# A twenty-chunk ring for the channel mixers' activations in a hybrid GLA/FoX trunk on one Trainium2 core

## The chip, the cores and the metric

The kernel runs on one core of one Trainium2 chip, in one launch. Its time is in device microseconds (us); three runs gave 2291.82 us in the median (2291.04 to 2292.42). The core's engines are TensorE (PE; PEld is its weight load), VectorE (DVE), ScalarE (ACT), GpSimd (POOL) and SyncE (SP). Here SP issues the weight loads and POOL the transfers of the channel mixers' activations.

## The reference

A decoder trunk of two layers over 256 tokens with a width of 2048. Layer 0 mixes tokens with gated linear attention, layer 1 with forgetting attention; both also attend to 256 memory tokens. After either comes a channel mixer, which is what the change touches:

```python
def causal_dwconv(u, w, b):
    s_ = u.shape[1]
    up = jnp.pad(u, ((0, 0), (CONV_WIDTH - 1, 0), (0, 0)))
    return w[0] * up[:, 0:s_] + w[1] * up[:, 1:s_ + 1] + w[2] * up[:, 2:s_ + 2] + b

def conv_ffn(h, w_up, conv_w, conv_b, w_down):
    u = causal_dwconv(h @ w_up, conv_w, conv_b)
    a, val = split_cols(u, [FFN_HIDDEN, FFN_HIDDEN])
    return (jax.nn.silu(a) * val) @ w_down
...
        h = rmsnorm(x, norm_ffn[i])
        x = x + conv_ffn(h, ffn_w_up[i], ffn_conv_w[i], ffn_conv_b[i], ffn_w_down[i])
```

The hidden width is 5632, which is 44 chunks of 128 for the activated half `a` and 44 for `val`.

## The kernel before

**Precision.** Every float32 operand is split in two fp32r parts, a high one (a ScalarE cast) and a low one (a VectorE subtraction). A product is three matmuls: high by high, low by high, high by low. `split_unit` (line 214) does this to the weights: SP loads a unit of 128 x 1024 values (512 KB) into one of four `raw` buffers, ScalarE makes `whi` (line 230), VectorE makes `wlo` (line 231). The cast and the subtraction have their place in their engine's order well ahead of the matmuls (`high_priority(offset=AHEAD)`).

**Panels.** A panel is a block of columns of a weight matrix, consumed unit by unit. There are three ways to run one. `panel_tm` (line 313) is *narrow*: 512 columns, two 128-row chunks of the contraction to a unit, 12 matmuls of 128 x 512, two accumulators. `proj_tm` (line 276) does the same with other orders of the last units. `pair_tm` (line 353) is *wide*: 1024 columns, one contraction chunk to a unit, 12 matmuls, four accumulators (two halves of the tokens by two halves of the columns). In a wide panel a pair of contraction chunks can be done by the Strassen-Winograd scheme with seven products for eight: two units in 21 matmuls for 24, with extra casts (`split_more`, its cast in line 349), subtractions of weights (lines 399 to 402), a sum of the source made beforehand (`token_sums`, tiles `usum` and `dsum`), and an evacuation of four extra banks (`early`). A wide panel uses all eight PSUM banks if it has a Strassen pair; `flip` exchanges the four that its last units write (tiles `acc`) with the four others (`ps_o`, `ps_s`, `ps_t`), so that the following panel finds four free.

**The mixer** (`ffn`, line 1329). The 44 chunks come in three `PARTS`: 0 to 15, 16 to 31, 32 to 43. For each part the up panels run first, then the part's down panels, which add into the residual `x[0]` to `x[3]` (four column quarters of 512). An up pair (`up_pair`) is a wide panel that yields four chunks of both halves; its contraction has 16 chunks, its Strassen pair is the input chunks 4 and 5 (`SEVEN_UP`). Parts 0 and 1 are made of four up pairs each; part 2 of up pairs 32 and 36 and two narrow panels 40 and 42 (`up`), whose accumulators ScalarE evacuates at line 1440. The down panels of parts 0 and 1 are two wide ones with 16 units, Strassen pairs at the part's chunks 4 and 10 (`SEVEN_DOWN`); those of part 2 are one wide panel of 12 units without a Strassen pair for quarters 0 and 1, then a narrow one each for quarters 2 and 3 (`add_out`).

**A chunk's way from up to down** (`turn`). When an up panel ends, VectorE adds the last parts (line 1429) and transposes 32 x 32 blocks (line 1393). POOL writes the tile to DRAM (`far`, line 606) and reads it back in another order, four transfers per tile (line 611). Then six *steps* follow for every two chunks: four of three taps each (ScalarE, lines 1348 to 1350), one that adds them (VectorE, line 1357, and silu, line 1358), one that gates, splits into high and low part and, where needed, makes the sums for a Strassen pair (`gated`: VectorE line 1365, ScalarE line 487, VectorE line 488). The steps wait in a list, `waiting`. They are due eight ticks of a clock after the evacuation (seven in narrow panels), and `tick(most)` is called after every unit and issues at most `most` that are due: alternately one and two in up pairs, two in narrow and down panels. A down panel issues all that are left by its last units. Taps are placed behind the latest weight cast, gatings behind the latest low part (`issue_after`).

**Where the chunks lie.** In layer 0 the mixer's input is in `bufB` and its sixteen activation chunks in `bufA`; in layer 1 the other way round. A part's chunk j goes to buffer j - lo, so a part's activations overwrite those of the part before, and its up panels' steps come behind the earlier part's down panels.

**The order on the engines** is not only that of the code: the program is built with a planner that simulates times (`schedule_with_timeline_sim=True`) and orders each engine's instructions by simulated readiness and priority. On the chip each engine then runs its list in order.

**Around the mixers.** Layer 0's mixer is followed by `fox`: the finished quarters of `x` are transposed, written to DRAM by SP and read back (`land`), and split (`take`) as input of the next projections; in the mixer's last panel `land` and `take` come after its third, fourth, fifth and sixth unit. `mk[1]` and `mv[1]`, the memory keys and values of layer 1 (128 x 1024 float32 each), are made at the kernel's start and read in `fox` by `mem_parts(1, "B")`. In layer 1 the last mixer is followed by the final norm.

## Time and profile before

| | |
|---|---|
| median of three runs | 2291.82 us |
| the profiled execution | 2289.51 us |
| its span, first to last instruction | 2287.7 us |
| mean granted TensorE clock | 0.990 |
| busy: PE / DVE / ACT / POOL | 2230.5 / 1790.0 / 1416.9 / 124.3 us |
| matmuls | 10317 |
| DMA | 513.37 MB, 224 GB/s over the span |

The mixers take about 458 to 1190 us (layer 0) and 1525 to 2280 us (layer 1). In a row of windows the columns are: the window, its length, then for PE, PEld, DVE, ACT and POOL the busy time and (x) the number of instructions that lie in it, the granted TensorE clock, the busy share of the DMA engines, GB/s. In a row of the timeline: start, duration, engine, line, operation, out<-in, shapes, count, and in brackets the engine's idle time before it and what ended it. In a row of waits: who waited, for whom, us in total, how often, the longest. Names such as `A`, `B` and `mix` are the buffers of inputs and activations; `fvt`, `temp`, `yu`, `yzu` and `turn` are tiles on the chunks' way.

### The profile page before, as it was taken

The numbers are of one execution on the slowest core, as the hardware profiler recorded it, in microseconds if no ns is written. First come the engines' busy times: TensorE is split into PE (matmuls) and PEld (weight loads), VectorE is DVE, ScalarE is ACT, GpSimd is POOL, SyncE is SP. The second block draws the span as 40 slices with busy tenths as digits, with TensorE's granted clock in tenths as the row PEclk, the third lists the DMA queues.
The fourth block names the chain that finished last, engine by engine and source line by source line (L and its number), as shares of the span: only waits on it lengthen the run. The fifth ranks groups of instructions, "written<-read, shape, count | busy, mean of one in ns | idle before, by whom it ended". The sixth has DMA issues, their size and how long they took to land. (4 is left out here: it accounts for less than half of the span.)

```text
span 2287.7 us, 30031 instructions
## 1 busy us (share of the span) xinstructions
PE 2230.5 (97%) x10317; PEld 1861.7 (81%) x10317; DVE 1790.0 (78%) x2639; ACT 1416.9 (62%) x2258; POOL 124.3 (5%) x235
## 2 busy tenths in 40 slices
PE   9999999999999999999999999999999999999997
PEld 7888888878778887788778998887777888778885
DVE  7769986688898789878677569677888878987866
ACT  6655665557865676656665455455876567765674
POOL 0000000001000001000100000000000000100110
PEclk9999999999999999999999999999999999999998
DMA  9776658867675776656777767676776577756673
GB/s 350 224 224 212 207 178 257 248 224 229 229 241 175 231 253 229 189 202 222 227 240 247 215 203 246 206 245 214 234 240 217 183 230 247 239 193 220 223 257 129
DMA packets 166593, 513.37 MB, mean 224 GB/s; under 512 B 20636, under 2 KB 43816, under 8 KB 166440
## 3 DMA queue, kind: packets, MB, share of 16 engines
q1 hardware_dynamic: 151080, 464.51, 62.5%
q0 software_dynamic: 14784, 46.15, 6.4%
q8 instruction: 81, 1.33, 0.2%
q10 hardware_dynamic: 576, 0.79, 0.1%
q14 instruction: 72, 0.59, 0.1%
HBM read 468.63 MB, written 42.74 MB: 224 GB/s over the span
## 5 line engine op out<-in xcount | busy, mean ns | idle before, releaser
L231 DVE TENSOR_TENSOR wlo<-raw,whi 128x1024 fp32r<-128x1024 f32 (+4 forms) x734 | 866.9, 1196 | 321.8 <-ACT whi L230 300.4
L230 ACT ACTIVATE whi<-raw 128x1024 fp32r<-128x1024 f32 (+4 forms) x734 | 746.9, 1036 | 464.6 <-PE acc L334 183.9
L334 PE MATMUL acc<-whi,B 128*128 128x512 f32 (+3 forms) x1376 | 323.8, 372 | 0.0
L334 PEld LDWEIGHTS acc<-whi,B 128*128 128x128 f32 x1376 | 251.2, 188 | 32.9
L349 ACT ACTIVATE whi<-raw 128x1024 fp32r<-128x1024 f32 (+1 forms) x144 | 136.6, 952 | 208.3 <-PE acc L374 73.4
L374 PE MATMUL acc<-whi,mix 128*128 128x512 f32 x850 | 222.9, 396 | 9.4 <-ACT fvt L1440 3.9
L350 DVE TENSOR_TENSOR wlo<-raw,whi 128x1024 fp32r<-128x1024 f32 (+1 forms) x144 | 155.7, 1084 | 67.5 <-ACT whi L349 61.5
L374 PE MATMUL acc<-whi,B 128*128 128x512 f32 x730 | 191.9, 395 | 11.1 <-ACT B L487 9.3
L374 PEld LDWEIGHTS acc<-whi,mix 128*128 128x128 f32 x850 | 161.6, 191 | 45.2 <-ACT fvt L1440 4.3
L334 PE MATMUL acc<-wlo,B 128*128 128x512 f32 (+3 forms) x688 | 176.1, 371 | 0.0
L374 PEld LDWEIGHTS acc<-whi,B 128*128 128x128 f32 x730 | 138.6, 191 | 42.0 <-ACT B L487 10.1
L334 PEld LDWEIGHTS acc<-wlo,B 128*128 128x128 f32 x688 | 126.7, 188 | 16.9
L1357 DVE TENSOR_TENSOR tap<-tap,tap 128x1024 f32<-128x1024 f32 x88 | 107.5, 1221 | 28.6 <-ACT tap L1349 20.2
L374 PE MATMUL acc<-wlo,mix 128*128 128x512 f32 x425 | 123.2, 395 | 0.1
L374 PE MATMUL acc<-wlo,B 128*128 128x512 f32 x365 | 106.0, 393 | 0.1
L374 PEld LDWEIGHTS acc<-wlo,mix 128*128 128x128 f32 x425 | 81.0, 191 | 17.8 <-DVE wlo L350 0.7
L374 PE MATMUL ps_s<-whi,B 128*128 128x512 f32 x342 | 93.8, 390 | 0.0
L374 PE MATMUL ps_s<-whi,mix 128*128 128x512 f32 x334 | 93.1, 391 | 0.0
L334 PE MATMUL acc<-whi,mix 128*128 128x512 f32 x336 | 84.1, 390 | 0.0
L374 PEld LDWEIGHTS acc<-wlo,B 128*128 128x128 f32 x365 | 69.2, 190 | 15.0 <-DVE wlo L350 0.5
L374 PEld LDWEIGHTS ps_s<-whi,B 128*128 128x128 f32 x342 | 64.2, 188 | 13.5
L374 PEld LDWEIGHTS ps_s<-whi,mix 128*128 128x128 f32 x334 | 63.0, 189 | 13.4
(425 smaller groups left out, 3783.1 us busy)
## 6 DMA issues: line engine op xcount, KB each, us to landing
raw<-wp SPq DMA_DIRECT2D x743, 512.0 KB, 4.6
raw<-wp SPq DMA_DIRECT2D x32, 384.0 KB, 3.5
far<-yu POOLq DMA_DIRECT2D x22, 512.0 KB, 3.8
far<-yzu POOLq DMA_DIRECT2D x22, 512.0 KB, 3.8
fvt<-far POOLq DMA_DIRECT2D x80, 128.0 KB, 3.0
yzu<-far POOLq DMA_DIRECT2D x80, 128.0 KB, 3.5
raw<-wp SPq DMA_DIRECT2D x24, 388.0 KB, 3.9
far<-blk SPq DMA_DIRECT2D x12, 512.0 KB, 4.9
```

Source lines behind the costliest of these rows:

```text
L230: casts.append(S.activation(hi[:, s], raw[:, s], AF.Copy))
L231: lows.append(V.tensor_tensor(lo[:, s], raw[:, s], hi[:, s].bitcast(F32), ALU.subtract))
L334: mm = TE.matmul(acc[b][:, :n], src[kc - base][:, part, b * P : (b + 1) * P], ready[low][:, j * n : (j + 1) * n], start=i == low == part = ...
L349: casts.append(S.activation(hi[:, :n], src, AF.Copy))
L350: lows.append(V.tensor_tensor(lo[:, :n], src, hi[:, :n].bitcast(F32), ALU.subtract))
L374: r = TE.matmul(bank[name], x, w, start=name not in begun, stop=last)
L1357: V.tensor_tensor(t, t, taps[n][:, :, :, :T], ALU.add)
```

## The change

The activations get twenty buffers for sixteen: chunk j goes to buffer j modulo 20. In layer 1 the four added ones are new tiles. In layer 0 they are the tiles of `mk[1]` and `mv[1]`: POOL writes these to DRAM (`parked`) before the mixer, and at the start of `fox` reads them back into the same places.

The order of the panels changes. After part 0's last up pair the first up pair of part 1 runs, then the two down panels of part 0; after part 1's last pair the first of part 2, then part 1's down panels. Up pairs and down panels are generators now, driven one unit at a time; after every unit of either alternately one or two steps are issued, and the rule that issues all that are left is gone. In part 2 the narrow up panels 40 and 42 become a wide up pair 40. Its down panels are interleaved by hand: eight units of the wide one, four of the narrow one for quarter 2, the last four of the wide one, the last two of the narrow one; quarter 3 follows as before. The Strassen pair of up panels moves from input chunks 4, 5 to 6, 7.

```diff
-WIDE = ((0, 4, 8, 12), (16, 20, 24, 28), (32, 36))
-SEVEN_UP = (4,)
+RING = 20
+SEVEN_UP = (6,)
...
+            for t, tag, far in ((mk, "mk1", parked[0]), (mv, "mv1", parked[1])):
+                t[1] = const.tile(list(t[1].shape), F32, name=tag + "again", tag=tag)
+                nc.gpsimd.dma_start(t[1].rearrange("p a b -> p (a b)"), far)
...
-            def gated(i, seven):
+            def gated(j):
...
-                        split(m, i + s, r[:, s, :])
-                    if seven:
-                        sums[i] = held("dsum", i)
-                        token_sums(r, sums[i])
+                        split(m, (j + s) % RING, r[:, s, :])
+                    if j < PARTS[-1][0] and j % 16 in SEVEN_DOWN:
+                        sums[j] = held("dsum", j % 16)
+                        token_sums(r, sums[j])
...
-                for f in (0,) if end else (0, 2):
-                    count[2] += 1
-
-                    def hook(k):
-                        tick(2)
-                        if k in (hi - lo - 5, hi - lo - 3):
-                            left = 6 if k == hi - lo - 5 else 0
-                            while len(waiting) > left:
-                                waiting.pop(0)[1]()
-                        if end and k == 6:
-                            getattr(then, "begin", int)()
-
-                    down_pair(l, p, f, m, {} if end else sums, count[2] % 2, pool, lambda: (temps(0), temps(1)),
-                              hook, then if end else None)
-                sums.clear()
-            add_out(("down", l, len(PARTS) - 1), m, then=then, first=2, spare=spare, last=last)
+            def drive(steps, most=lambda k: 1 + clock[0] % 2):
+                for k in steps:
+                    tick(most(k))
+
+            for k in SEVEN_UP:
+                input_sums(k)
+            for k in up_pair(0):
+                first(k)
+            done = 4
+            for p, (lo, hi) in enumerate(PARTS[:-1]):
+                while done < hi + 4:
+                    drive(up_pair(done))
+                    done += 4
+                src = [m[c % RING] for c in range(lo, hi)]
+                for f in (0, 2):
+                    count[2] += 1
+                    drive(down_pair(l, p, f, src, {c - lo: t for c, t in sums.items()}, count[2] % 2, pool,
+                                    lambda: (temps(0), temps(1))))
+                sums.clear()
+            lo, hi = PARTS[-1]
+            while done < hi:
+                drive(up_pair(done))
+                done += 4
+            p = len(PARTS) - 1
+            src = [m[c % RING] for c in range(lo, hi)]
+            wide = down_pair(l, p, 0, src, {}, 0, pool, lambda: (temps(0), temps(1)), then)
+
+            def third(b, a):
+                add_to(2)(b, a)
+                then(2, b)
+
+            single = panel_tm(("down", l, p, 2), src, third)
+            for _ in range(8):
+                next(wide)
+                tick(2)
+            getattr(then, "begin", int)()
+            for u in range(4):
+                single(u)
+                tick(2)
+            assert not waiting
+            for _ in wide:
+                pass
+            for u in range(4, 6):
+                single(u)
+            add_out(("down", l, p), src, then=then, first=3, spare=spare, last=last)
...
+            more = []
+            for t, tag in ((mk, "mk1"), (mv, "mv1")):
+                parked.append(dram.tile([P, 4 * T], F32, name="park" + tag, tag="park" + tag, bufs=1))
+                nc.gpsimd.dma_start(parked[-1], t[1].rearrange("p a b -> p (a b)"))
+                more.append(const.tile([P, 2, 2, T], F32R, name="more" + tag, tag=tag))
+            ffn(0, n, bufB, bufA + [t[:, i] for t in more for i in range(2)], ys, turned3, ys, then, tp, temps)
...
+        more = [op.tile([P, 2, T], F32R, name=f"more{i}") for i in range(RING - KC)]
+        ffn(1, n, bufA, bufB + more, ys, zs, zs, then, op, temps, spare, last)
```

More of the change, by code (lines that the diff above doesn't have):

```diff
@@ L87, in ffn @@
         for p, (lo, hi) in enumerate(PARTS):
-            for j in range(lo, hi, 2):
-                if j in WIDE[p]:
-                    cols = [(c + (j + i) * P, 2 * P) for i in (0, 2) for c in (0, HID)]
-                    out.append((("up", l, j), ("ffn_w_up", l), full, cols, 1))
-                elif j - 2 not in WIDE[p]:
-                    tm(("up", l, j), ("ffn_w_up", l), j * P, 2 * P, more=[(HID + j * P, 2 * P)])
+            for j in range(lo, hi, 4):
+                cols = [(c + (j + i) * P, 2 * P) for i in (0, 2) for c in (0, HID)]
+                out.append((("up", l, j), ("ffn_w_up", l), full, cols, 1))
             last = p == len(PARTS) - 1
@@ L351, in split_more, with pair_steps @@
         return hi, lo
-    def pair_tm(units, src, sums, flip, pool, early, late, hook):
+    def pair_steps(units, src, sums, flip, pool, early, late):
         bank = {}
@@ L1280, in fox, with down_pair @@
                     steps[f](u)
[L1283 removed]
+    def down_pair(l, p, f, src, sums, flip, pool, temps, then=None):
         def early(bank):
@@ L1300, in late @@
                 then(f + h, b)
-        pair_tm(where["down", l, p, f], src, sums, flip, pool, early, late, hook)
+        return pair_steps(where["down", l, p, f], src, sums, flip, pool, early, late)
     def add_out(key, src, then=None, spare=None, last=None, first=0, hooks=None, late=1):
@@ L1409, in tick, with up_pair @@
                         waiting.pop(0)[1]()
-            def up_pair(j, i, hook):
+            def up_pair(j):
                 count[2] += 1
-                turns = [turn(j + 2 * h_, i + 2 * h_, 8) for h_ in range(2)]
+                turns = [turn(j + 2 * h_, 8) for h_ in range(2)]
                 u = {}
@@ L1430, in late @@
                     turns[h_](b, u[b, h_])
[L1432 to L1443 removed]
+                return pair_steps(where["up", l, j], h, up_sums, count[2] % 2, pool, early, late)
             def first(k):
```

37 lines of the change are left out of this document (6 added, 31 removed).

## The prediction

> **What bounds the kernel now.** I read the page's engine shares first, then TensorE's waits, then a row of 25 us windows laid over the two channel mixers, then single rows of the timeline where a window falls short.
>
> ```profile
> span 2287.7 us, 30031 instructions
> PE 2230.5 (97%) x10317; PEld 1861.7 (81%) x10317; DVE 1790.0 (78%) x2639; ACT 1416.9 (62%) x2258; POOL 124.3 (5%) x235
> ```
> ```profile
> PE acc L374 <- ACT B L487: 9.3, 2, 6.5
> PE acc L374 <- ACT whi L349: 8.2, 6, 1.6
> PE acc L374 <- ACT A L487: 4.6, 2, 2.8
> PE ps_s L374 <- ACT whi L349: 4.2, 3, 2.8
> PE acc L374 <- ACT fvt L1440: 3.9, 1, 3.9
> PE acc L374 <- ACT mix L487: 3.9, 1, 3.9
> PE ps_t L374 <- ACT whi L349: 3.0, 5, 1.6
> PE ps_o L374 <- DVE wlo L231: 2.6, 1, 2.6
> ```
> The kernel is a stream of matmuls that is rarely broken, so only holes in that stream are worth time. The waits are of three kinds. L487 is the split of a finished activation chunk (a down panel has come to a chunk that is not ready), L349 the cast of a Strassen pair's weights, L1440 the evacuation of a narrow up panel.
>
> How much each hole costs is counted, not added from idle times, because matmuls are slower after a hole. An undisturbed 25 us window counts 111 matmuls (first row), one per 25/111 = 0.225 us; every matmul fewer in a row below is 0.225 us lost.
>
> ```profile
> 2050.00:2075.00 25.00, 25.00 (x111) 20.63 (x111) 21.97 (x27) 12.04 (x13) 0.00 (x0) 1.00 0.65 237
> 455.00:480.00 25.00, 22.16 (x93) 16.97 (x92) 20.66 (x48) 14.08 (x25) 0.14 (x2) 1.00 0.52 167
> 595.00:620.00 25.00, 23.48 (x103) 18.97 (x102) 22.75 (x28) 18.00 (x29) 5.49 (x10) 1.00 0.59 193
> 655.00:680.00 25.00, 21.85 (x87) 16.67 (x86) 22.55 (x29) 19.46 (x35) 0.00 (x0) 0.93 0.51 173
> 860.00:885.00 25.00, 23.48 (x104) 18.98 (x103) 22.75 (x28) 18.03 (x29) 5.49 (x10) 1.00 0.59 195
> 922.00:947.00 25.00, 19.75 (x70) 14.31 (x69) 20.99 (x26) 19.89 (x37) 0.00 (x0) 0.86 0.47 156
> 1119.00:1144.00 25.00, 21.07 (x87) 17.02 (x86) 16.37 (x19) 16.36 (x27) 3.96 (x8) 0.93 0.63 178
> 1150.00:1175.00 25.00, 21.12 (x83) 16.98 (x82) 16.65 (x20) 15.49 (x38) 0.00 (x0) 0.86 0.48 170
> 1535.00:1560.00 25.00, 21.73 (x85) 16.50 (x84) 18.44 (x41) 11.87 (x23) 0.00 (x0) 0.93 0.45 148
> 1630.00:1655.00 25.00, 24.34 (x105) 19.17 (x104) 23.86 (x30) 18.01 (x29) 5.50 (x10) 1.00 0.66 224
> 1675.00:1700.00 25.00, 23.49 (x103) 18.95 (x103) 22.42 (x28) 18.61 (x31) 5.49 (x10) 1.00 0.60 191
> 1740.00:1765.00 25.00, 19.66 (x73) 15.37 (x72) 23.35 (x31) 16.09 (x28) 0.00 (x0) 0.86 0.47 163
> 1945.00:1970.00 25.00, 23.49 (x103) 18.94 (x103) 21.65 (x26) 19.82 (x34) 5.49 (x10) 1.00 0.65 215
> 2005.00:2030.00 25.00, 21.60 (x85) 16.39 (x84) 24.15 (x30) 18.37 (x31) 0.00 (x0) 0.93 0.48 176
> 2197.00:2222.00 25.00, 24.01 (x106) 19.56 (x106) 17.15 (x18) 16.63 (x27) 3.94 (x8) 1.00 0.79 248
> 2228.00:2253.00 25.00, 18.48 (x75) 14.84 (x74) 16.52 (x20) 16.48 (x37) 0.00 (x0) 0.86 0.40 138
> ```
> The first pair of matmul counts is TensorE's; the value before the DMA share is the granted clock. Missing, in matmuls: **A**, first down panels of parts 0 and 1 (655, 922, 1740, 2005): 24 + 41 + 38 + 26 = 129, or 29.0 us. **B1**, change to the last down panels (1119, 2197): 24 + 5 = 29, or 6.5 us. **B2**, last chunk pair of the last part (1150, 2228): 28 + 36 = 64, or 14.4 us. **C**, first up pair of each mixer (455, 1535): 18 + 26 = 44, or 9.9 us. **D**, Strassen pair in a later up pair (595, 860, 1630, 1675, 1945): 8 + 7 + 6 + 8 + 8 = 37, or 8.3 us. In all 303 matmuls, 68.2 us: the most that filling holes in the mixers can give.
>
> **Part by part. A, the next part's up pair ahead of the down panels.** In the first mixer the down panels of part 0 begin at 636.10 (first matmul on acc from mix). The last up pair ended there, and its four chunks go through transposes, a write to DRAM and back, 24 taps and two gatings. These are ready 35 and 45 us later:
>
> ```profile
> 636.10 1.98 PE L374 MATMUL acc<-whi,mix 128*128 128x512 f32 x8
> ```
> ```profile
> 671.01 0.71 ACT L487 ACTIVATE A<-cv 128x256 fp32r<-128x256 f32 x2
> ```
> ```profile
> 671.47 3.53 PE L374 MATMUL acc<-whi,A 128*128 128x512 f32 x8 [2.76 <-ACT A L487]
> ```
> ```profile
> 681.38 0.73 ACT L487 ACTIVATE A<-cv 128x256 fp32r<-128x256 f32 x2 [0.69 <-DVE cv L1365]
> ```
> Unit 12 of the panel wants the first of them after 12 x 12 matmuls less 2 x 3 for two Strassen pairs, 138 x 0.225 = 31 us: the 2.76 us wait. After the change a whole up pair (16 x 12 - 3 = 189 matmuls, 42.5 us) stands ahead, so a chunk is wanted 73 us after its up pair and the L487 wait cannot come. That part goes for certain: 20 of the 24 matmuls at 655 and 22 of 26 at 2005 (4 are left to the Strassen casts), 4.5 + 5.0 us.
>
> The other two places are not the same hole:
>
> ```profile
> 921.12 0.60 ACT L1348 ACTIVATE tap<-fvt,cw 128x256 f32<-128x256 f32 x1 [3.35 <-DMA fvt<-far]
> ```
> ```profile
> 934.77 1.22 PE L374 MATMUL ps_t<-whi,dsum 128*128 128x512 f32 x2 [1.56 <-ACT whi L349]
> ```
> ```profile
> 1747.17 2.07 PE L374 MATMUL ps_s<-whi,dsum 128*128 128x512 f32 x4 [2.76 <-ACT whi L349]
> ```
> ```profile
> 1761.17 0.80 PE L374 MATMUL ps_o<-wlo,mix 128*128 128x512 f32 x1 [2.58 <-DVE wlo L231]
> ```
> There ScalarE runs its queue in order: a tap waits 3.35 us for its landing, the casts of the panel's second Strassen pair (chunks 10, 11) stand behind it and behind the other taps, and TensorE waits for the casts. After the change the same panel has the taps of the next part's first pair in the same place: due eight ticks after the evacuation, that is from unit 6 on, before as after. What differs is the pace, at most 1.5 steps per unit for 2, so twelve steps take eight units instead of six. The gain lies between nothing (the collision stays) and all of it. I take half at 922, to which the second of the two waits in the row "A L487: 4.6, 2, 2.8" also belongs (1.8 us), and a quarter at 1740, where both waits are for casts: 4.6 + 2.1 us. A: 16.2 us, bounds 9.5 to 29.0.
>
> **B1.** The wait at 1133.01 is for an evacuation by the narrow up panels, on a ScalarE blocked by a tap's landing.
>
> ```profile
> 1128.57 1.71 ACT L1349 ACTIVATE tap<-turn,cw 128x256 f32<-128x256 f32 x4 [5.18 <-DMA turn<-far]
> ```
> ```profile
> 1133.01 1.22 PE L374 MATMUL acc<-whi,mix 128*128 128x512 f32 x2 [3.93 <-ACT fvt L1440]
> ```
> Chunks 40 to 43 become a wide pair, L1440's code is gone, and the wide down panel that follows takes the four work banks while that up pair drains the others: 6.5 us. Bounds 0 (another evacuation is late) to 6.5. The wide pair also has a Strassen pair, three matmuls fewer in each mixer: 6 x 0.225 = 1.4 us.
>
> **B2.** Now the last chunks are wanted after 10 units (27 us) and come late:
>
> ```profile
> 1161.75 3.78 PE L374 MATMUL acc<-whi,mix 128*128 128x512 f32 x8 [3.88 <-ACT mix L487]
> ```
> After it, eight wide units and four of the third panel come first, 12 x 12 matmuls or 32.4 us, then two more units before 42 and 43, 37.8 us. The chain above needs 35 and 45 us with Strassen work on ScalarE and VectorE beside it, which these panels do not have. With 35 the wait is 2.6 us, and the second, 45 - 37.8 - 2.6, some 4.6; without that work beside it both may be near nothing. I take 3 us lost in each mixer for 7.2 now: gain 8.4, bounds 0 to 14.4.
>
> **C.** The Strassen pair of the inputs moves from chunks 4, 5 to 6, 7, so its weights are wanted two units (5.4 us) later. The waits at 455 and 1535 are for those casts (L349), whose weights land late; I take 6 of the 9.9 us. The two loads are queued behind the loads of two more units on SP, so not all; bounds 0 to 9.9.
>
> **D.** Pairs that follow an up pair with taps open are 16 instead of 14 (up 4, 8, 12, 16, 24, 28, 32, 40 for 4, 8, 12, 20, 24, 28, 36, in each mixer). 8.3/14 = 0.6 us each makes 9.5: a loss of 1.2. But the Strassen pair now stands at units 6 and 7, where the taps come due, and not at 4 and 5; the taps are ordered behind the latest cast, which speaks for the small number. Bounds: a gain of 8.3, and a loss of 16 x 1.8 - 8.3 = 20.5 if each pair stalls as at 1675.
>
> **The moves that I cost at nothing.** Two tiles of memory keys and values go to DRAM and back on POOL's queue, four transfers of 512 KB like this one:
>
> ```profile
> far<-yu POOLq DMA_DIRECT2D x22, 512.0 KB, 3.8
> ```
> ```profile
> 1322.28 0.61 ACT L642 ACTIVATE kv<-mk 128x512 fp32r<-128x512 f32 x1
> ```
> The first reader comes 160 us after the mixer's last wait at 1161.75, which covers the way back; the ring's seventeenth chunk is written five up pairs (5 x 42.5 us) after the way out. Uncovered they would cost 4 x 3.8 = 15 us. In the first mixer's end three output quarters (0, 1, 2) now finish within some 7 us instead of 0 and 1 a panel earlier, and quarter 0 is asked back on SP with the loads queued behind it. That read stands five units (5 x 12 x 0.225 = 13.5 us) after the quarter, for nine (24.3 us) before, and a write of a quarter takes
>
> ```profile
> far<-blk SPq DMA_DIRECT2D x12, 512.0 KB, 4.9
> ```
> so it may hold SP between 0 and 4.9 us; I take 1.5. Gating, taps, casts and evacuations are otherwise the same in number, except one Strassen pair per mixer, on engines that do not bound there (VectorE 16.37 of 25 us at 1119).
>
> **Sum.** 16.2 + 6.5 + 1.4 + 8.4 + 6.0 - 1.2 - 1.5 = 35.8 us off the profiled execution's 2289.5 (span 2287.7 and 1.8 around it): 2253.7. The median shown is 2.3 us above that execution, so 2256.
>
> **A rule of the skill.** The window at 1740 has a granted clock of 0.86 after idle times of 2.76 and 2.58 us. The Trainium skill (TensorE: Matmul & The Clock Gate, Why this matters for your kernels) says that idle gaps up to some 3 us leave the clock alone. By it the holes at 655 and 2005 would be worth their idle time, 2.8 us each, and the sum 4 us less, an estimate of 2260; these rows contradict it.
>
> **The rivals.** (1) *All holes close*: the slower pace also frees the Strassen casts, C and B2 go whole: 29.0 + 6.5 + 14.4 + 9.9 + 1.4 = 61.2, 2231. For it: the up pairs already run at this pace, and D is small there. Against it: 1740 is a loss without any late chunk. (2) *Only the late chunks go*: casts keep colliding at 922 and 1740, the first pairs still wait, and the end's wait stays with four chunks due at once: 9.5 + 6.5 + 1.4 - 1.2 - 1.5 = 14.7, 2277. For it: ScalarE's queue is in order and its total work unchanged. (3) *The Strassen pair at units 6 and 7 meets the taps, slower*: it waits as at 1740 in each of the 16 pairs, one of that place's two idle times each, half of 8.6 us: 16 x 4.3 = 69 for the 9.5 of D, so 2256 + 59 = 2315. It decides from (35.8 + 9.5)/16 = 2.8 us per pair on. For it: 921.12; against: the order of taps behind the casts. (4) *It does not do what it says*: the order on each engine comes from a planner's simulated times; if that already pulls work into these holes, or pulls the up pair's units back behind the down units, the wait stays, 2290.
>
> **Chances.** Forecast 0.50, (1) 0.15, (2) 0.20, (3) 0.10, (4) 0.05. The range 2229 to 2284 holds the forecast, (2) and most of (1). A measurement of this kernel tells 0.2%, 4.6 us, from no change. Faster 0.85, within that bound 0.04, slower 0.11.
>
> **What would show it.** A: no TensorE wait for L487 in the first down panels of parts 0 and 1; L349 waits there of under 2 us. B1: no group at the narrow evacuation. B2: one L487 wait of 1 to 4 us per mixer. C: first pairs with at least 100 matmuls per 25 us. D: about 9 us in the up pairs. The taps of the next part's first pair inside the first down panel. Wrong, if L349 waits in up pairs exceed 20 us together, if a wait for the tiles brought back shows in the second layer, or if the up pair does not stand ahead of the down panels.

## The result, and the profile after

The changed kernel takes 2283.74 us (median of 9 runs, 2280.40 to 2286.24), the kernel before, in runs beside it, 2291.04 us (9 runs). The ratio is 0.997, 95% interval 0.996 to 0.9981: 7 us faster, a fifth of the 35.8 us forecast. The profiled execution after took 2282.04 us.

In the profile after, the old helpers stand two lines higher: L374 of before is L372, the casts L230 and L349 are L228 and L347, the low parts L231 and L350 are L229 and L348, the split of a chunk L487 is L485, the narrow panels' L334 is L332. The taps moved down by one (now L1349 to L1351, their adds L1358, the silu of the gating L1359, its multiplication L1366). L496 is the split of an input chunk of the next layer.

The page, its span and engine shares; then TensorE's waits (who waits for whom, us in total, times, longest):

```profile
span 2280.0 us, 30080 instructions
PE 2229.1 (98%) x10311; PEld 1852.6 (81%) x10311; DVE 1806.4 (79%) x2667; ACT 1421.8 (62%) x2264; POOL 127.0 (6%) x239
```
```profile
PE acc L372 <- ACT whi L347: 18.2, 18, 2.2
PE ps_o L372 <- ACT mix L485: 8.9, 2, 4.9
PE acc L372 <- ACT whi L228: 4.2, 9, 0.9
PE acc L332 <- ACT B L496: 2.3, 1, 2.3
```
The waits for a chunk in the first down panels (2.8, 1.8 and 2.8 us in the groups `A` and `B` of L487 before) are gone; only the two at the mixers' ends are left, on `ps_o`. So is the narrow evacuation, L1440. In their place stands one large group, the Strassen casts (L347): 18.2 us, and 1.7 us more on `ps_t`, against 17.6 before for all L349 rows together (8.2 + 4.2 + 3.0 + 2.2). Of the 18.2 us, 17.5 lie in the four first down panels. And ordinary casts (L228), which TensorE never waited for in the mixers before, cost 4.2 us on `acc` and 1.6 us on `ps_o`.

Where these stand, by windows (PE, PEld, DVE, ACT, POOL busy with counts, granted clock, DMA share, GB/s). The four 50 us rows are the first down panels of parts 0 and 1; an undisturbed 50 us holds 220 or 221 matmuls (a row further down).

```profile
455.00:480.00 25.00, 25.00 (x112) 20.61 (x111) 23.52 (x51) 16.23 (x29) 0.14 (x2) 1.00 0.66 217
1125.00:1150.00 25.00, 25.00 (x112) 20.71 (x111) 14.75 (x17) 12.60 (x20) 5.51 (x10) 1.00 0.87 277
1150.00:1175.00 25.00, 20.95 (x86) 16.72 (x85) 19.12 (x22) 17.59 (x33) 0.00 (x0) 0.93 0.51 164
1190.00:1215.00 25.00, 21.95 (x94) 17.16 (x93) 24.09 (x63) 18.16 (x40) 0.89 (x2) 1.00 0.93 286
1535.00:1560.00 25.00, 25.00 (x111) 20.30 (x110) 20.46 (x36) 14.70 (x20) 0.00 (x0) 1.00 0.60 198
2228.00:2253.00 25.00, 20.11 (x77) 15.97 (x76) 18.46 (x22) 17.43 (x31) 0.00 (x0) 0.86 0.52 164
...
680.00:730.00 50.00, 45.15 (x187) 35.42 (x186) 43.32 (x52) 31.79 (x51) 5.51 (x10) 0.97 0.57 182
948.00:998.00 50.00, 45.02 (x194) 35.47 (x193) 44.82 (x56) 34.16 (x55) 5.51 (x10) 1.00 0.63 210
1752.00:1802.00 50.00, 44.67 (x184) 35.05 (x183) 42.53 (x51) 31.91 (x51) 5.51 (x10) 0.97 0.58 181
2021.00:2071.00 50.00, 45.02 (x180) 34.56 (x178) 42.23 (x52) 32.07 (x51) 5.52 (x10) 0.93 0.62 196
```
The first up pairs (455, 1535) and the way into the last panels (1125) are full now. The first down panels are as leaky as before: 745 matmuls where 882 fit, 137 x 0.225 = 30.8 us, against 29.0. The ends (1150, 2228) miss 25 + 34 = 59, or 13.3 us, against 14.4. And the landing between the layers (1190), full before, has a hole.

What stands in a leaky panel shows in the timeline of the first one, VectorE and ScalarE (start, duration, engine, line, operation, shapes, and in brackets the idle time before and what ended it), then TensorE. The up pair ahead of it ended at 675.10, where the panel begins.

```profile
674.81 1.40 DVE L1429 SCALAR_TENSOR_TENSOR fvt<-acc,ny,fvt 128x512 f32<-128x512 f32 x2
676.13 1.40 DVE L1429 SCALAR_TENSOR_TENSOR temp<-acc,ny,temp 128x512 f32<-128x512 f32 x2
677.45 1.22 DVE L1358 TENSOR_TENSOR tap<-tap,tap 128x1024 f32<-128x1024 f32 x1
678.58 1.30 DVE L1393 STREAM_TRANSPOSE yu<-fvt 128x512 f32<-128x512 f32 x2
...
682.63 0.70 DVE L1393 STREAM_TRANSPOSE yu<-temp 128x512 f32<-128x512 f32 x1
683.26 0.65 DVE L348 TENSOR_TENSOR wlo<-raw,whi 128x512 fp32r<-128x512 f32 x1
683.83 1.21 DVE L1358 TENSOR_TENSOR tap<-tap,tap 128x1024 f32<-128x1024 f32 x1
...
685.13 0.63 ACT L1359 ACTIVATE tap<-tap 128x512 f32<-128x512 f32 x1 [4.24 <-DVE tap L1358]
687.42 0.73 ACT L485 ACTIVATE A<-cv 128x256 fp32r<-128x256 f32 x2 [1.65 <-DVE cv L1366]
688.10 1.06 ACT L347 ACTIVATE whi<-raw 128x1024 fp32r<-128x1024 f32 x1
...
705.76 0.63 ACT L1359 ACTIVATE tap<-tap 128x512 f32<-128x512 f32 x1 [3.89 <-DVE tap L1358]
707.32 0.60 ACT L1288 ACTIVATE fvt<-acc 128x512 f32<-128x512 f32 x1 [0.93 <-PE acc L372]
707.82 1.05 ACT L347 ACTIVATE whi<-raw 128x1024 fp32r<-128x1024 f32 x1
```
```profile
689.21 1.20 PE L372 MATMUL acc<-whi,dsum 128*128 128x512 f32 x4 [1.00 <-ACT whi L347]
...
708.92 1.20 PE L372 MATMUL acc<-whi,dsum 128*128 128x512 f32 x4 [1.16 <-ACT whi L347]
...
712.86 0.73 PE L372 MATMUL acc<-whi,dsum 128*128 128x512 f32 x2 [1.70 <-ACT whi L347]
```
At 675 the second gating of part 0's last up pair is still open: the last of its tap adds (L1358) stands on VectorE behind the evacuations and transposes of the pair that ran ahead, until 683.83; ScalarE's silu waits 4.24 us for that add; and the cast of the panel's first Strassen pair stands behind the silu, so TensorE waits. Twenty us later the same happens to the second Strassen pair, now with the gating of the pair that ran ahead (705.76). Each of the four panels has both holes, of 1.7 to 6.7 us.

### The profile page after: what moved, and what is told of

It reads as the page before. It is cut to its first block, busy times and chain, and to the rows that moved or that the text cites. A ratio compares the mean times of both kernels' runs of the same rounds, so it can differ in the third digit from the quotient of the medians.

```text
span 2280.0 us, 30080 instructions
## 1 busy us (share of the span) xinstructions
PE 2229.1 (98%) x10311; PEld 1852.6 (81%) x10311; DVE 1806.4 (79%) x2667; ACT 1421.8 (62%) x2264; POOL 127.0 (6%) x239
## 4 chain that ended last, share of the span: by engine, by line
PE 75%; issue 11%; DVE 4%; ACT 4%; DMA 4%; POOL 1%; SPq 0%; ACTq 0%; DVEq 0%; POOLq 0%
PE acc L372 22%; PE acc L332 21%; PE ps_s L372 11%; PE ps_o L372 6%; PE ps_t L372 5%; PE acc L259 3%; PE acc L304 3%; PE ps_s L332 2%; PE acc L257 1%; DMA yzu<-far 1%; DMA raw<-wp 1%; ACT whi L228 1%; DVE wlo L229 1%; DVE wlo L348 1%; DMA fvt<-far 1%
## 5 line engine op out<-in xcount | busy, mean ns | idle before, releaser
L229 DVE TENSOR_TENSOR wlo<-raw,whi 128x1024 fp32r<-128x1024 f32 (+4 forms) x730 | 860.9, 1193 | 328.4 <-ACT whi L228 308.2
L228 ACT ACTIVATE whi<-raw 128x1024 fp32r<-128x1024 f32 (+4 forms) x730 | 743.1, 1036 | 443.4 <-PE acc L332 164.5
L332 PE MATMUL acc<-whi,B 128*128 128x512 f32 (+3 forms) x1264 | 297.1, 370 | 3.1 <-ACT B L496 2.3
L347 ACT ACTIVATE whi<-raw 128x1024 fp32r<-128x1024 f32 (+1 forms) x152 | 144.5, 953 | 218.3 <-PE acc L372 74.2
L332 PEld LDWEIGHTS acc<-whi,B 128*128 128x128 f32 x1264 | 229.8, 188 | 32.9 <-ACT B L496 3.3
L348 DVE TENSOR_TENSOR wlo<-raw,whi 128x1024 fp32r<-128x1024 f32 (+1 forms) x152 | 164.0, 1087 | 62.7 <-ACT whi L347 55.3
L372 PE MATMUL acc<-whi,B 128*128 128x512 f32 x792 | 202.9, 390 | 1.9 <-ACT whi L228 1.9
L372 PE MATMUL acc<-whi,mix 128*128 128x512 f32 x764 | 196.8, 391 | 2.3 <-ACT whi L228 2.3
L372 PEld LDWEIGHTS acc<-whi,B 128*128 128x128 f32 x792 | 148.2, 188 | 34.9 <-ACT whi L228 4.0
L372 PEld LDWEIGHTS acc<-whi,mix 128*128 128x128 f32 x764 | 142.8, 188 | 34.8 <-ACT whi L228 4.9
L332 PE MATMUL acc<-wlo,B 128*128 128x512 f32 (+3 forms) x632 | 161.3, 369 | 0.0
L332 PEld LDWEIGHTS acc<-wlo,B 128*128 128x128 f32 x632 | 116.1, 188 | 14.8
L1358 DVE TENSOR_TENSOR tap<-tap,tap 128x1024 f32<-128x1024 f32 x88 | 107.3, 1219 | 17.8 <-ACT tap L1350 12.9
L372 PE MATMUL acc<-wlo,B 128*128 128x512 f32 x396 | 111.9, 390 | 0.0
L372 PE MATMUL acc<-wlo,mix 128*128 128x512 f32 x382 | 108.4, 390 | 0.0
L372 PE MATMUL ps_s<-whi,mix 128*128 128x512 f32 x360 | 104.2, 401 | 0.0
L372 PE MATMUL ps_s<-whi,B 128*128 128x512 f32 x348 | 95.7, 391 | 0.0
L372 PEld LDWEIGHTS acc<-wlo,B 128*128 128x128 f32 x396 | 74.2, 188 | 16.0 <-DVE wlo L229 0.6
L372 PEld LDWEIGHTS acc<-wlo,mix 128*128 128x128 f32 x382 | 71.5, 188 | 15.7 <-DVE wlo L229 0.7
L372 PEld LDWEIGHTS ps_s<-whi,mix 128*128 128x128 f32 x360 | 70.1, 195 | 15.2
L372 PE MATMUL ps_o<-whi,mix 128*128 128x512 f32 x218 | 71.7, 402 | 10.0 <-ACT mix L485 8.9
L372 PEld LDWEIGHTS ps_s<-whi,B 128*128 128x128 f32 x348 | 65.6, 189 | 13.9
```

What stands on the lines that cost most here:

```text
L228: casts.append(S.activation(hi[:, s], raw[:, s], AF.Copy))
L229: lows.append(V.tensor_tensor(lo[:, s], raw[:, s], hi[:, s].bitcast(F32), ALU.subtract))
L332: mm = TE.matmul(acc[b][:, :n], src[kc - base][:, part, b * P : (b + 1) * P], ready[low][:, j * n : (j + 1) * n], start=i == low == part = ...
L347: casts.append(S.activation(hi[:, :n], src, AF.Copy))
L348: lows.append(V.tensor_tensor(lo[:, :n], src, hi[:, :n].bitcast(F32), ALU.subtract))
L372: r = TE.matmul(bank[name], x, w, start=name not in begun, stop=last)
```

## The experiments

Every kernel was timed beside the kernel before; the ratios are those. The kernel before took 2285.3 us beside e1 to e4, 2289.9 beside e5 to e8 and about 2288 beside e9 to e14, so kernels of different groups are compared by ratio. To see where each kernel loses time I added, for each hole in TensorE's stream inside the mixers, by how much the distances between the starts of successive matmuls exceed the undisturbed 0.227 us (holes over 0.6 us):

| us lost in | before | after | e1 | e7 | e9 | e10 |
|---|---|---|---|---|---|---|
| first down panels (A) | 30.1 | 31.6 | 13.0 | 16.7 | 0 | 0 |
| way into the last panels (B1) | 6.9 | 0 | 0 | 0 | 0 | 0 |
| last chunks (B2) | 14.8 | 13.9 | 6.0 | 6.0 | 5.2 | 0 |
| first up pairs (C) | 10.0 | 0 | 9.5 | 0 | 0 | 0 |
| later up pairs and the rest (D) | 8.5 | 13.9 | 10.5 | 9.3 | 11.1 | 12.6 |
| landing between the layers | 0 | 3.9 | 7.7 | 6.6 | 6.4 | 7.8 |
| all | 70.3 | 63.3 | 46.7 | 38.6 | 22.7 | 20.4 |
| span of the profile | 2287.7 | 2280.0 | 2264.4 | 2257.5 | 2240.0 | 2239.4 |

The differences of the sums follow those of the spans within 2 us, so nothing large is missing from the table. Row D holds two things: holes at the up pairs' Strassen casts (8.5 us before, 3.8 after, 10.5 in e1) and, after alone of these kernels, 8.9 us of small holes at the ordinary casts (L228) of the two units behind the Strassen pair, where ScalarE has a run of taps ahead of the cast (nine from 828.50 to 832.39, for one). Another 1.2 us after lie in the second down panels.

**e1, the Strassen pair of the up panels back at 4, 5.** The rest of the change stays.

```diff
-SEVEN_UP = (6,)
+SEVEN_UP = (4,)
```


> The changed kernel with the Strassen pair of the up panels back at input chunks 4, 5. Theory S (the pair at chunks 6, 7 pushes an up pair's steps 5 us later, so that the last of them run into the first Strassen pair of the down panel, and TensorE waits there): the first hole of each first down panel (3.8, 2.1, 3.6, 1.7 us of lost matmul time in the changed kernel) closes, while the first up pairs' holes of before (9.9 us) come back; together about 2283, within 4 us of the changed kernel. Rival P (the slower pace of one and a half steps per unit makes the hole): the holes in the down panels stay and the first up pairs' holes come back: about 2293.

Measured 2264.61 us, ratio 0.9913 (0.9899 to 0.9926), 0.0057 or 13 us better than the change, more than either theory had. The first up pairs lose their 9.5 us again, but the first down panels lose 18.6 us less, and the last chunks 7.9 us less. The timeline of e1 at the same place, VectorE and ScalarE (the panel begins at 679.27):

```profile
676.82 0.61 ACT L1359 ACTIVATE tap<-tap 128x512 f32<-128x512 f32 x1
...
678.75 1.41 DVE L1429 SCALAR_TENSOR_TENSOR fvt<-acc,ny,fvt 128x512 f32<-128x512 f32 x2
...
681.87 0.71 ACT L485 ACTIVATE A<-cv 128x256 fp32r<-128x256 f32 x2
684.05 1.06 ACT L347 ACTIVATE whi<-raw 128x1024 fp32r<-128x1024 f32 x1 [1.47 <-issue]
```
The silu now comes ahead of the evacuations, 2.5 us before the panel instead of 10 us into it, and the cast waits for nobody. The same windows of e1:

```profile
680.00:730.00 50.00, 49.07 (x216) 40.01 (x215) 46.80 (x59) 34.86 (x56) 5.50 (x10) 1.00 0.64 226
945.00:995.00 50.00, 47.30 (x200) 38.20 (x200) 44.27 (x56) 32.21 (x51) 5.50 (x10) 0.97 0.59 211
1748.00:1798.00 50.00, 49.06 (x216) 40.00 (x215) 46.79 (x58) 33.93 (x55) 5.49 (x10) 1.00 0.63 217
2006.00:2056.00 50.00, 47.45 (x193) 37.78 (x192) 42.88 (x53) 31.27 (x50) 5.50 (x10) 0.93 0.55 187
```
57 matmuls missing of 882, 12.8 us. All that is left there belongs to the second Strassen pair; the first pair's holes are gone in all four panels.

**e2, the kernel before with its pair at 6, 7.**

```diff
-SEVEN_UP = (4,)
+SEVEN_UP = (6,)
```


> The kernel before with only the Strassen pair of the up panels at chunks 6, 7. If this move alone closes the holes in the first up pair of each mixer and costs nothing elsewhere: 2291 - 10 = 2281, below the changed kernel. Theory S: it gains 10 in the first up pairs and loses about as much in the other up pairs and in the first Strassen pair of the down panels: 2283 to 2291.

2291.13 us, ratio 1.0029 (1.0019 to 1.004). By the same count the first up pairs go from 10.0 to 1.3 us, and the first down panels from 30 to 41: the move takes more than it gives in the old order too.

**e3, no up pair ahead.** The rest of the change stays; the panels issue two steps per unit, so that the last pair's chunks are ready in time.

```diff
-                while done < hi + 4:
+                while done < hi:
...
-                                    lambda: (temps(0), temps(1))))
+                                    lambda: (temps(0), temps(1))),
+                          lambda k: 2)
```


> The changed kernel without the run ahead: a part's down panels follow its last up pair at once, with two steps per unit; the ring, the wide last up pair and the interleaved end stay. If the run ahead gains what the waits for late chunks cost before (14 to 16 us of the down panels' holes): slower than the changed kernel by 10 to 16 us, 2294 to 2300. If the run ahead only turns these waits into waits for Strassen casts: within 4 us of the changed kernel.

2294.14 us, ratio 1.0042 (1.0029 to 1.0055). Against the change's 0.997 the pair ahead, with the pace, is worth 0.0072 or 16 us, as the first theory had it.

**e4, steps held back during the first down panel (f = 0)**, one per unit in the second.

```diff
-                                    lambda: (temps(0), temps(1))))
+                                    lambda: (temps(0), temps(1))),
+                          lambda k, f=f: 1 if f else 0)
```


> The changed kernel, with the steps of the pair that runs ahead held back: none is issued in the part's first down panel, one per unit in the second. Theory T (the second hole of each first down panel, 4.0, 4.3, 4.7 and 6.7 us, comes from this pair's taps standing among the casts of the Strassen pair at chunks 10, 11): these holes close, 2283.7 - 17 = 2267, down to 2272 if the taps disturb the second panel a little. Rival: the collision only moves to the second panel's Strassen pairs: within 4 us of the changed kernel.

2264.76 us, ratio 0.9915 (0.9901 to 0.9928), 0.0055 or 13 us better than the change, near the lower end of what its theory had. Two of the four windows of e4:

```profile
680.00:730.00 50.00, 48.36 (x204) 39.09 (x203) 45.10 (x54) 28.62 (x38) 5.49 (x10) 0.97 0.66 232
2021.00:2071.00 50.00, 48.87 (x212) 39.33 (x211) 44.92 (x51) 33.72 (x45) 4.23 (x8) 1.00 0.66 224
```
Here it is the other half that goes: the second Strassen pair's holes are gone in all four panels, the first pair's are left (3.8, 3.6, 2.1 and 1.7 us), since the steps that spill over from the up pair are issued already. Two causes in one panel, and each of e1 and e4 takes one.

**e5, the old pace.** Two steps per unit in the down panels: `lambda k: 2` at the same place.

> The changed kernel with two steps per unit in the down panels of parts 0 and 1 for one and a half. Rival P (the slower pace makes the holes in the first down panels): they shrink by 8 us or more, 2276 or less. Theory S with T (place of the Strassen pairs against the steps, the pace does not matter): within 4 us of the changed kernel.

2284.12 us, ratio 0.9975 (0.9965 to 0.9984): the change's own 0.997. The slower pace, on which the forecast rested half of 922 and a quarter of 1740, does nothing.

**e6, the reload of the parked tiles later in the program.**

```diff
-            for t, tag, far in ((mk, "mk1", parked[0]), (mv, "mv1", parked[1])):
...
+            with tc.issue_after(lows[-1].ins):
+                for t, tag, far in ((mk, "mk1", parked[0]), (mv, "mv1", parked[1])):
...
             for j, (lo, hi) in enumerate(FV_PARTS):
```


> The changed kernel, with the two tiles of memory keys and values read back after the first projections of the second layer and not at their start. If the read back is what delays the weights and the landing of the quarters between the layers (2.6 + 1.2 us of holes there): these holes close, 4 us less, 2280. Rival (the quarters finish too close together, so that the read back of a quarter stands just behind its write): no change there, within 2 us.

2283.58 us, ratio 0.9972 (0.9962 to 0.9983), the landing as before. But it tells nothing of the reload: POOL issued it at 1188.37 for 1185.28, in both right after the last matmul that reads the tile, 45.7 us idle before. The edit moved the text and not the transfer; e13 does it properly.

**e7, the pair at 6, 7 in the first up pair only, at 4, 5 in all others.** The sums of chunks 4 and 5 are made after the first pair, in the same tile.

```diff
-SEVEN_UP = (6,)
+SEVEN_UP = (6, 4)
...
-                up_sums[k] = held("usum", k)
+                up_sums.clear()
+                up_sums[k] = held("usum", 0)
...
-            for k in SEVEN_UP:
-                input_sums(k)
+            input_sums(SEVEN_UP[0])
             for k in up_pair(0):
                 first(k)
+            input_sums(SEVEN_UP[1])
```


> The changed kernel with the Strassen pair at chunks 6, 7 in each mixer's first up pair alone and at 4, 5 in all others (the sums are made anew in the same tile). Theory S: what the pair at 4, 5 gained in the run before (2264.6) and the first pairs' holes closed as in the changed kernel (9.5 us less): 2255 to 2258. If the sums made anew are late: no better than 2262.

2259.22 us, ratio 0.9866 (0.9848 to 0.9884). The windows of e7 at the first pairs:

```profile
455.00:480.00 25.00, 25.00 (x111) 20.62 (x111) 23.04 (x53) 15.42 (x26) 0.14 (x2) 1.00 0.63 200
1535.00:1560.00 25.00, 25.00 (x112) 20.46 (x111) 21.15 (x33) 17.24 (x23) 0.00 (x0) 1.00 0.67 205
```
The place 6, 7 is worth its 10 us where the weights land late (0.9866 against e1's 0.9913 is 10.8 us), and costs where taps run. Together this is the change with its one bad term undone: 30.7 us off the kernel before.

**e8, more cover at the end.** In layer 1 four units of quarter 3 are run ahead of the wide panel's last four too.

```diff
+            if last is not None:
+                quarter = panel_tm(("down", l, p, 3), src, last)
+                for u in range(4):
+                    quarter(u)
             for _ in wide:
                 pass
             for u in range(4, 6):
                 single(u)
+            if last is not None:
+                for u in range(4, 6):
+                    quarter(u)
+                return
```


> The changed kernel; in layer 1's end four units of the panel for quarter 3 also come before the last four units of the wide one (that panel is then a plain narrow one). Cover for the last chunks grows from 32.4 to 43.2 us. If the chain of the last chunks takes 38 us as the row of the changed kernel says: the hole of 8.0 us there closes, less 1 to 3 us for the final norm that no longer overlaps the panel: 2277 to 2279. Rival (that chain is held by the casts of the cover itself, so that it grows with it): the hole stays, 2284 to 2287.

2278.58 us, ratio 0.9952 (0.9938 to 0.9966). The hole of 8.0 us at the end of layer 1 is gone (the window 2215 to 2240 is full: 25.00 us busy). The other mixer's 5.5 us stay.

**e9, e10: e7 with the steps held back (e4), then with the cover (e8) too.**

> The kernel with the Strassen pair at 6, 7 in the first up pairs alone (2259.2), and the steps of the pair that runs ahead held back to the second down panel. Theory T: its holes at the second Strassen pair of the first down panels (4.7, 5.9, 1.2, 4.9 us) close: 2243 to 2248. If they only move to the second panel: 2256 to 2262.

> The same, and the longer cover at layer 1's end: 3 to 5 us less than the run before it, as between the changed kernel and its version with the cover (5.2 us). If that hole depends on what went before it: no change.

e9: 2242.6 us, ratio 0.9795 (0.978 to 0.9809). e10: 2239.93 us, 0.9782 (0.9768 to 0.9796), the fastest of all, 2.2% below the kernel before. The cover is worth 2.7 us here, less than the 3 to 5 expected and than the 5.2 us hole that it closes, since 1.4 us come back at the landing and 1.5 in row D. Two windows of e9, which are also the measure of an undisturbed 50 us:

```profile
680.00:730.00 50.00, 50.00 (x221) 41.17 (x220) 43.92 (x53) 28.91 (x37) 5.49 (x10) 1.00 0.67 229
2003.00:2053.00 50.00, 50.00 (x220) 40.85 (x219) 43.69 (x51) 33.11 (x50) 0.00 (x0) 1.00 0.67 231
```
With both causes taken away nothing is lost in the first down panels: 0.9866 to 0.9795 is 16.3 us, and e7 had 16.7 us of holes there.

**e11, e10 with the third panel cut otherwise in layer 0**: two of its units instead of four ahead of the wide panel's last four, and four behind; as many steps in all.

```diff
-            for u in range(4):
+            begun = 2 if last is None else 4
+            for u in range(begun):
                 single(u)
-                tick(2)
+                tick(8 // begun)
...
-            for u in range(4, 6):
+            for u in range(begun, 6):
                 single(u)
```


> The same, and in layer 0's end two units of the third panel ahead of the wide one's last four and four behind, for four and two: the quarters 0 and 1 are then done two units earlier against the third panel's end. Theory L (the holes between the layers, 4.7 + 1.9 us, come from quarters that finish too close to the next projections): 2 to 4 us less. Rival: the last chunks of layer 0 are then late, and a hole of the same size opens there: no change.

2244.19 us, ratio 0.9801 (0.9787 to 0.9815), 4 us slower than e10 beside it; the rival's hole at the last chunks came, and more. The landing loses 4.1 us for 7.8, since the quarters end further apart, but the last chunks have less in front of them: TensorE waits 4.1 us for one at the end of that mixer, a hole of 5.8 us.

**e12, e7 without the up pair ahead** (the edit of e3).

> The kernel with the Strassen pair at 6, 7 in the first up pairs alone (2259.2), without the run ahead and with two steps per unit in the down panels. If the run ahead is worth the waits for late chunks that the prediction counted (9.5 to 16 us): 2269 to 2275. If what helped was the place of the Strassen pairs alone: 2257 to 2262.

2268.41 us, ratio 0.9907 (0.9891 to 0.9923). Against e7 the pair ahead is worth 0.0041, 9 us; so even without it two thirds of e7's gain are there, from the first up pairs, the wide last pair and its order.

**e13, e14: the landing.** Both are e10 with the reload held by data: a one-column copy on VectorE, which needs the forget gates of the second layer, writes each tile ahead of it. e14 also sends the quarters to DRAM and back on POOL's queue instead of SP's (the last two lines below are e14's alone).

```diff
-            for t, tag, far in ((mk, "mk1", parked[0]), (mv, "mv1", parked[1])):
-                t[1] = const.tile(list(t[1].shape), F32, name=tag + "again", tag=tag)
-                nc.gpsimd.dma_start(t[1].rearrange("p a b -> p (a b)"), far)
...
                 V.tensor_tensor_scan(cs, ones[:, 0:1].to_broadcast([P, T]), mz, 0.0, ALU.mult, ALU.add)
+                for t, tag, far in ((mk, "mk1", parked[0]), (mv, "mv1", parked[1])):
+                    t[1] = const.tile(list(t[1].shape), F32, name=tag + "again", tag=tag)
+                    V.tensor_copy(t[1][:, 0, 0:1], cs[:, 0:1])
+                    nc.gpsimd.dma_start(t[1].rearrange("p a b -> p (a b)"), far)
...
-                    away.append((f, far_away(far, flat(y), T)))
+                    away.append((f, far_away(far, flat(y), T, queue)))
```


> The best version so far (first pair at 6, the others at 4, steps held back in the first down panels, quarter 3 begun early in layer 1; 0.9782 of the kernel before), with the way back of the two parked tiles held by one added one-column copy each on VectorE that needs a result of the second layer's gates, some 20 us or more later. Theory S (the order of SP's queue makes the landing between the layers late: a load stands behind a write that waits for a transpose and behind a read-back): the holes of 2.96 and 4.88 us at the landing stay, 6 to 9 us together, ratio 0.977 to 0.980. Rival R (the reload's 1 MB fills the DMA engines, whose share is 0.98 there): the holes fall below 3 us together, ratio 0.975 to 0.977.

> The same as e13_reload_later, and the three quarters that go to DRAM and back between the layers use POOL's queue instead of SP's, so that no weight load stands behind them. Theory S: the holes at the landing fall below 3 us together, ratio 0.974 to 0.977, and ScalarE no longer waits 3 us or more for a load of weights there. Rival R (the DMA engines themselves are full there): the loads still land late, the holes stay at 6 us or more, ratio as for e13.

2240.32 us, 0.9791 (0.9778 to 0.9805), and 2240.14 us, 0.9788 (0.9775 to 0.9802): no gain from either. In e13 no reload is issued up to 1235, and the holes at the landing are 0.9 + 6.0 us. In e14 they are 5.2 + 1.4 us, and here the waits changed hands; ScalarE, TensorE and SP in e14's timeline:

```profile
1165.48 26.61 SPq L223 DMA_DIRECT2D raw<-wp  x8
...
1176.16 1.71 ACT L496 ACTIVATE B<-fvt,gains 128x256 fp32r<-128x256 f32 x4 [5.46 <-DMA fvt<-far]
...
1176.72 3.26 PE L332 MATMUL acc<-whi,B 128*128 128x512 f32 x7 [3.49 <-ACT B L496]
```
In e10 a load stood behind a quarter's write and read-back on SP (issued at 1165.55), landed 7.5 us later, and its cast (idle 5.77 us for it) held the split. In e14 no cast waits for a load any more, and the split waits for the read-back itself. So the reload does not set the time (R falls by e13), and the order of SP's queue alone does not either (S falls by e14).

What is left is the trip of a quarter out and back. From the issue of quarter 0's write to the landing of the last of its four parts it took 15.1 us in the kernel before, 12.3 in the change, 14.0 in e10, 12.1 in e13 and 15.5 in e14 (read from the landings in the traces). The trip is not longer than it was; what shrank is the cover, from nine units of matmuls (24.3 us) to five (13.5 us). e11, where the landing's holes nearly halve with the quarters further apart, agrees.

How much of the trip is the DMA engines' load stays open. Their busy share is 0.90 to 0.93 in e14's windows there, the weight loads issued from 1165.48 to 1171.99 took 6.9 to 8.6 us for a median of 4.6, and quarter 0's read-back 7.0 to 8.3 us for a median of 3.0 of that size on POOL's queue: the transfers are slow, as e14's R has it, though nothing waits for the loads. And on POOL's queue the read-back stands behind the next quarter's write and is issued 2.4 us after its own write has landed, so a queue's order still has a part. An order that covers both the landing and the last chunks of layer 0 was not found.

## Why the prediction was right or wrong

| term, us gained | forecast | measured in the change | with the pair at 4 after the first (e7) |
|---|---|---|---|
| A, first down panels | 16.2 | -1.5 | 13.4 |
| B1, way into the last panels | 6.5 | 6.9 | 6.9 |
| Strassen in the last pair | 1.4 | six matmuls fewer, 1.4 | 1.4 |
| B2, last chunks | 8.4 | 0.9 | 8.8 |
| C, first up pairs | 6.0 | 10.0 | 10.0 |
| D, later up pairs | -1.2 | -5.4 | -0.8 |
| landing | -1.5 | -3.9 | -6.6 |
| sum | 35.8 | 8.4 | 33.1 |

The measured columns are differences of rows in the table of holes, and stand within 3 us of those of the spans (7.7 and 30.2). That the time still lies inside the range, just below its end of 2284, is luck: C gave 4.0 us more than forecast, for its own reason.

**The step that failed is D's**: "the Strassen pair now stands at units 6 and 7, where the taps come due", and its price was looked for in the 16 up pairs alone, with a loss of 1.2 us between bounds of +8.3 and -20.5. The up pairs with the rest of that row lost 5.4 us. What was put at nothing is what stands behind the pair. The steps come later by some 8 us: from an up pair's evacuation (L1429) to the multiplication of its second gating (L1366), in the last up pair of a part, it is 53.6 to 53.9 us in the change and 44.6 to 46.8 in e1 and e7. First the change, then e1, VectorE:

```profile
632.84 0.75 DVE L1429 SCALAR_TENSOR_TENSOR fvt<-ps_o,ny,fvt 128x512 f32<-128x512 f32 x1 [0.68 <-PE ps_o L372]
...
686.70 0.69 DVE L1366 TENSOR_TENSOR cv<-tap 128x512 f32<-128x512 f32 x1
```
```profile
634.33 0.74 DVE L1429 SCALAR_TENSOR_TENSOR fvt<-ps_o,ny,fvt 128x512 f32<-128x512 f32 x1
...
680.07 0.68 DVE L1366 TENSOR_TENSOR cv<-tap 128x512 f32<-128x512 f32 x1
```
An up pair takes 42.5 us, and what does not fit spills into the panel that follows. Behind the last pair of a part that is the first down panel with its first Strassen pair (A); behind wide pair 40 it is the end, where that pair's own chunks are due (B2): their first split, wanted 32.5 us after the pair, comes 36.4 us after it in layer 0, for 32.0 in e1 and e7, and 37.8 us in layer 1, for 36.7 and 36.9. e1, e2 and e7 show it: with that one place undone A is 13.4 for 16.2, B2 8.8 for 8.4, D -0.8 for -1.2, the whole gain 30.7 us. Rival 3 had the mechanism ("meets the taps, slower") but its place and price wrong, 69 us in the up pairs. The sign named for it, over 20 us of waits for Strassen casts in the up pairs, did not show, because those waits came in the down panels.

**A in detail.** That the waits for chunks (L487) go "for certain" held: none is left in these panels. That what is left at 655 and 2005 is small did not: "4 are left to the Strassen casts" became 27 to 40 missing matmuls per panel. Nor was the collision at 922 and 1740 eased: the pair ahead's taps stand between the second pair's casts in all four panels, which the forecast had as "the same place as before" for two of them, at half and a quarter of the price. It took the pace as what differs; e5 shows that the pace is nothing. e4 and e9 show the collision by closing it, 16.3 us from e7 to e9. The L349 waits there were to be "under 2 us"; 2.2 us is the longest, but there are 18 on `acc` (16 of them in these panels), and the holes are longer than the waits: 31.6 us of holes for 17.5 us of waits on `acc`.

**B1** was right in kind and size. **C** was right in kind and too small: the two units' delay covers the late weights whole. **B2** failed in the change by D's step; even in e7 layer 1 keeps a wait of 3.3 us, in the 1 to 4 us forecast (the change has 4.1 and 4.9). e8 shows that it is cover that is missing: four more units in front close it.

**The landing** was named and mis-sized: 1.5 us for 3.9, and up to 7.8 once the rest runs smoothly. The step gave the price to SP's queue, "hold SP between 0 and 4.9 us"; e14 shows that without that queue nearly as much is lost (6.6 us for 7.8). A trip of 12 to 16 us, the write and the read-back together, stood against five units, 13.5 us, and that should have been priced, and not the queue alone.

**The reload and the parking**, costed at nothing, cost nothing that shows: e13 holds the reload back past 1235 and the ratio stays, and in the change's trace nothing waits for the way out, issued at 96 us.

**The clock after a hole.** After an idle time of 2.35 us (TensorE at 1200.93 below) the window's clock is 1.00 and the hole costs 2.6 us; after the 2.76 us at 1747.17 of the kernel before (with 2.58 us more 14 us later) it is 0.86, and the first of the two holes costs 4.6. So the rule of the Trainium skill (TensorE: Matmul & The Clock Gate, Why this matters for your kernels), to keep idle gaps under some 3 us, is borne out only in part here: shorter gaps can slow the clock too. Counting matmuls instead of idle times was right.

```profile
1200.93 1.89 PE L332 MATMUL acc<-whi,B 128*128 128x512 f32 x7 [2.35 <-ACT B L496]
```

## What to carry to other kernels

When an operation is moved inside a repeated stage, cost what it pushes out of the stage's end as well as what it meets inside: steps that no longer fit into the stage come out on whatever follows it, and an in-order engine queues that stage's own casts behind them. A place that is right for one instance (the first pair, whose weights land late, where no taps run) can be wrong for the others; choose it for each. And work that is run ahead brings its own follow-up work with it: say where that is issued, and hold it back from the panel whose casts it would meet.

## What the runs showed that was not expected

The price of idle time on TensorE jumps, and not at one length. Single idle times of 0.93 to 1.6 us made holes of 1.2 to 1.9 us, hardly more than themselves, at a clock of 1.00; two of 1.77 and 0.93 us within 4 us of one another (second Strassen pair in e1, at 968) made 4.7 us, and 4.9 us of idle time at the end of layer 1 made 8.0 us:

```profile
2235.00 0.80 PE L372 MATMUL ps_o<-whi,mix 128*128 128x512 f32 x1 [4.89 <-ACT mix L485]
```
The slowed matmuls behind such a hole follow 0.43 us after one another for 0.227. In between, both happen. The first row, of e9 (with 0.39 us more a moment later), made a hole of 4.6 us at a clock of 0.93 over 25 us; the second, of e5, a hole of 3.2 us at a clock of 1.00:

```profile
1173.75 0.73 PE L332 MATMUL acc<-whi,B 128*128 128x512 f32 x2 [2.07 <-ACT B L496]
```
```profile
2056.53 1.68 PE L372 MATMUL acc<-whi,dsum 128*128 128x512 f32 x6 [2.98 <-ACT whi L347]
```
So the length of an idle time alone does not tell its price between some 1.8 and 3 us; what else decides was not tested. Two short waits close together can cost as much as a long one.
